# A hybrid decoder layer on one core: FF2's weight sums move into the stage of q and gates, rows and u stores change tiles and queues

## The chip, the cores and the metric

The kernel runs on one core of one Trainium2 chip. The time is device microseconds for one launch. Lower is better. Engines are named as in the profile: PE (TensorE), DVE (VectorE), ACT (ScalarE), POOL (GpSimd), SP (SyncE, which here only issues DMAs).

## The reference, cut to what matters

One layer on 2048 prompt tokens and 8 x 4 sampled tokens, width 1024, FF width 4096, all in float32:

```python
h = _rmsnorm(x, n1)
z = h @ w_in                                   # 1024 x 4864
hq, hf, hi, hg, sq, sk, sv, ga, gb = split(z)
y_a = (hgrn2(hq, hf, hi) normed * silu(hg)) @ w_up_a
y_b = sliding_window_attention(rot(sq), rot(sk), sv, sinks) @ w_up_b
m = sigmoid(ga) * y_a + sigmoid(gb) * y_b
x = x + m @ w_o
h2 = _rmsnorm(x, n2)
x = x + square(relu(h2 @ w_ff1)) @ w_ff2       # 1024 x 4096, 4096 x 1024
y = _rmsnorm(x, normf_w)
```

## The kernel before, in words

**Products.** Each float32 operand is split into a rounded high part (a cast on ACT, line 230) and a low part (a subtraction on DVE, line 231), and a product is three matmuls: high x high, high x low, low x high. A weight tile `r_...` of 128x1024 is loaded by SP's queue into the ring `w` (`wtile`, 12 tiles), and its parts `h_...` and `l_...` take two more tiles of it. The ring serves all of the kernel that needs a 128x1024 tile for a short time.

**Tokens.** Four blocks b0 to b3 of 512 tokens make two superblocks, sb0 (b0, b1) and sb1 (b2, b3; the samples ride along, so its halves have 528 columns in two chunks of 264). For each superblock the program has these stages:

1. Norm tiles (`norm_tile`): rows of x are normed, transposed on PE, and the transposed rows `hw` are kept for the even block in the slots `hT` (split) and written to DRAM as `hraw` for both.
2. `skv` and `sq`: keys, values and queries of attention for the even block (`colN`, `colN512`), staged in tiles `zqkb` and stored to DRAM (`zqk`). `sq` takes the eight rows of the weight in four steps of 24 matmuls; each step needs one `h_sqb` and one `l_sqb`.
3. The stage of q and gates (`strassen_T("z...")`): hq, gb and ga of both blocks at once by a seven-product Strassen scheme. Its operands: `hraw` comes back as `za11b` to `za22b` (ring `zs`), DVE forms `zs1b`, `zs2b` and differences, and these are split into the slots `zA`, `zS`. The weights `w1r_z` are loaded as 128x512 tiles, combined on DVE (lines 273 to 279) and split into `w1T_z`, `w1B_z`. A *unit* is one pair of columns of 128; there are ten. `a()` of a unit is its first two products (`fB`, `fC`), `b()` the next three (`fB`, `fD`, `fB`), `c()` the last two; a product is 12 matmuls. In sb0 the order is: `a` of units 0 to 5, `b` of unit 0, and then for each further unit `c` of the unit before and its own `b`, from unit 6 on with its own `a` ahead of both. Results are added up on DVE out of PSUM (lines 301, 314, 327, 335) and stored to DRAM (`z`) on the queues of POOL (q) and ACT (gates).
4. The even block: attention, HGRN2 with `hi`, `hf`, `hg`, gate b, gate a, then `wo`, and norm 2. The transposed rows `h2w` are written to `h2T`. During `wo` of the even block `reload` brings the odd half of `hraw` into `hT`. Then the odd block, with its own `sq` and `skv` at its head.
5. FF1 (`strassen_T("f...")`, 16 pairs): its results `u` are stored as seven operands for FF2 by `f1_fin`, on SP's queue.
6. FF2 in seven steps, whose weights are `w_ff` and four combinations of it, `w_T` (T1 to T4). The end forms the output rows (`Fin`: the final norm, tiles `nj` and `fx`).

**The weight sums.** The four combinations are made once, in sb0, by `w2_sums(i)` for i = 0 to 15: four loads of 128x512 (line 466, 256 KB each), four subtractions on DVE (lines 468 to 471), four stores (line 473). A ring `ws` of 5 tiles holds one sum; the fifth tile is the first difference. So the loads of sum i+1 wait until the stores of sum i have landed. In the program before, hooks in `sq` of b1, in the loops of the gates, and in the list of `reload` call them: they run from 285.8 to 556.6 us.

**The order of the work** on each engine is fixed when the program is built: a scheduler places the instructions by its own estimates, from the order of the code and the free tiles of the rings. At run time each engine and each queue takes its list strictly in order, so that an instruction that waits holds up all that stand behind it.

## Time and profile before

| what | value |
|---|---|
| three runs | 2969.36, 2987.56, 2986.71 us, median 2986.71 |
| profiled execution | 2976.32 us, its span 2974.5 us |
| mean granted TensorE clock | 0.979 |
| busy: PE, DVE, ACT, POOL | 95%, 60%, 40%, 10% |
| moved by DMA | 499 MB, mean 168 GB/s |

The profiled execution lies 10.4 us (0.35%) under the median of the three runs. The stages lie in it like this: norm tiles, skv and sq of sb0 up to about 84 us; the stage of q and gates 84 to 290; b0 to 507; sq and skv of b1 to 560; b1 to 790; FF1 to 1110; FF2 to 1459; sb1 the same way: sq of b2 and then the stage of q and gates from 1497 to 1703, b2 to 1940, b3 to 2278, FF1 to 2620, FF2 to the end. PE's busy time says little by itself, since a matmul at half clock counts double; the column PEclk goes with it.

### The profile page before, as it was taken

How to read it: one execution, taken by the hardware profiler on the slowest of the kernel's cores; microseconds unless marked ns; L12 is line 12 of the kernel's file. 1: busy time of each engine (PE TensorE's matmuls, PEld its weight loads, DVE VectorE, ACT ScalarE, POOL GpSimd, SP SyncE). 2: the span in 40 equal slices, each digit the busy share in tenths (PEclk: the TensorE clock that was granted, in tenths of full speed). 3: DMA queues.
4: the chain of work that ended last, by engine and by line, in shares of the span. 5: the costliest groups of instructions: out<-in, count | busy, mean ns of one | idle time of the engine just before them, and what ended most of it. 6: DMA issues, size and time to landing. Idle time of an engine off the chain costs nothing. (4 is left out here: it accounts for less than half of the span.)

```text
span 2974.5 us, 50416 instructions
## 1 busy us (share of the span) xinstructions
PE 2822.1 (95%) x20087; PEld 2444.8 (82%) x20087; DVE 1772.7 (60%) x2877; ACT 1179.3 (40%) x2257; POOL 291.3 (10%) x485
## 2 busy tenths in 40 slices
PE   5999998899999999999799999999998999999998
PEld 4877687777777888888699967777887999999998
DVE  4654785566677675545665457425756777654446
ACT  4434442434433344543343444234424333344433
POOL 4001011202200000010210010120012000000001
PEclk8999999999999999999899999999999999999999
DMA  7435757534644456665653423432256444485553
GB/s 238 156 121 167 231 192 268 182 97 139 217 162 152 154 196 237 228 214 191 214 150 106 140 93 98 155 123 87 84 182 187 152 144 155 141 284 199 176 194 107
DMA packets 417204, 499.08 MB, mean 168 GB/s; under 512 B 30636, under 2 KB 277448, under 8 KB 416952
## 3 DMA queue, kind: packets, MB, share of 16 engines
q1 hardware_dynamic: 380688, 411.12, 42.9%
q0 software_dynamic: 16448, 55.93, 5.7%
q10 hardware_dynamic: 19832, 28.79, 2.7%
q8 instruction: 158, 2.59, 0.4%
q14 instruction: 78, 0.64, 0.1%
HBM read 356.16 MB, written 140.61 MB: 167 GB/s over the span
## 5 line engine op out<-in xcount | busy, mean ns | idle before, releaser
L1324 PE MATMUL f<-f2S,hw2T 128*128 128x264 f32 (+1 forms) x576 | 184.1, 320 | 0.0
L1326 PE MATMUL f<-f2S,lw2T 128*128 128x264 f32 (+1 forms) x576 | 183.5, 319 | 0.0
L1325 PE MATMUL f<-f2S,hw2T 128*128 128x264 f32 (+1 forms) x576 | 183.5, 319 | 0.0
L155 DVE TENSOR_TENSOR lw2T<-lw2T,hw2T 128x1024 fp32r<-128x1024 f32 x64 | 78.1, 1223 | 121.1 <-ACT hw2T L154 120.7
L238 PE MATMUL fB_f<-S,w1T_f 128*128 128x264 f32 (+1 forms) x384 | 123.9, 323 | 6.0 <-DVE c_f L301 3.8
L1324 PE MATMUL f<-f2A,h_w2B 128*128 128x264 f32 (+1 forms) x384 | 123.3, 321 | 1.0 <-ACT f2A L154 1.0
L1325 PE MATMUL f<-f2A,h_w2B 128*128 128x264 f32 (+1 forms) x384 | 123.2, 321 | 0.9 <-DVE f2A L155 0.9
L240 PE MATMUL fB_f<-S,w1T_f 128*128 128x264 f32 (+1 forms) x384 | 123.0, 321 | 0.0
L239 PE MATMUL fB_f<-S,w1T_f 128*128 128x264 f32 (+1 forms) x384 | 122.9, 320 | 0.0
L1326 PE MATMUL f<-f2A,l_w2B 128*128 128x264 f32 (+1 forms) x384 | 122.7, 320 | 0.0
L154 ACT CAST hw2T<-lw2T 128x1024 fp32r<-128x1024 f32 x64 | 67.2, 1050 | 130.6 <-DMA lw2T<-w_T 128.7
L1324 PEld LDWEIGHTS f<-f2S,hw2T 128*128 128x128 f32 x576 | 108.4, 188 | 7.5 <-DVE hw_ab L410 0.3
L1325 PEld LDWEIGHTS f<-f2S,hw2T 128*128 128x128 f32 x576 | 108.4, 188 | 7.4
L1326 PEld LDWEIGHTS f<-f2S,lw2T 128*128 128x128 f32 x576 | 108.0, 188 | 7.6
L155 DVE TENSOR_TENSOR f2S<-f2S 128x1024 fp32r<-128x1024 f32 (+1 forms) x64 | 79.2, 1241 | 54.6 <-ACT f2S L154 53.5
L231 DVE TENSOR_TENSOR l_w2B<-rw2B,h_w2B 128x1024 fp32r<-128x1024 f32 x48 | 58.8, 1224 | 75.8 <-ACT h_w2B L230 69.9
L230 ACT CAST w1T_f<-w1r_f 128x512 fp32r<-128x512 f32 x128 | 76.4, 620 | 62.2 <-DVE w1r_f L275 29.5
L231 DVE TENSOR_TENSOR w1T_f<-w1r_f,w1T_f 128x512 fp32r<-128x512 f32 x128 | 85.9, 687 | 21.8 <-ACT w1T_f L230 21.4
L231 DVE TENSOR_TENSOR w1B_f<-w1r_f,w1B_f 128x512 fp32r<-128x512 f32 x96 | 65.4, 687 | 39.4 <-ACT w1B_f L230 38.5
L299 ACT COPY c_f<-fB_f 128x264 f32<-128x264 f32 (+1 forms) x80 | 36.0, 450 | 133.0 <-PE fB_f L240 130.3
L154 ACT CAST f2S<-f2S 128x1024 fp32r<-128x1024 f32 (+1 forms) x64 | 67.9, 1064 | 51.0 <-DMA f2S<-u_S 48.5
L191 PE MATMUL wob<-h_wob,m_b 128*128 128x512 f32 x192 | 76.6, 399 | 10.0 <-DVE ta_b L1023 10.0
(798 smaller groups left out, 9418.2 us busy)
## 6 DMA issues: line engine op xcount, KB each, us to landing
w1r_f<-w_ff SPq DMA_DIRECT2D x150, 256.0 KB
lw2T<-w_T SPq DMA_DIRECT2D x64, 512.0 KB
w1r_z<-w_in SPq DMA_DIRECT2D x102, 256.0 KB
rw2B<-w_ff SPq DMA_DIRECT2D x48, 512.0 KB
u_S<-s_f SPq DMA_DIRECT2D x128, 132.0 KB
f2S<-u_S SPq DMA_DIRECT2D x32, 528.0 KB
ws<-w_ff SPq DMA_DIRECT2D x64, 256.0 KB
r_wob<-w_o SPq DMA_DIRECT2D x32, 512.0 KB
```

What stands on the lines that cost most here:

```text
L154: nc.scalar.copy(hi, F(lo))
L155: nc.vector.tensor_tensor(lo, F(lo), F(hi), ALU.subtract)
L191: nc.tensor.matmul(ps[0:nr], lh, uh[:, kk, :], start=(k == 0), stop=False)
L230: nc.scalar.copy(dh, src)
L231: nc.vector.tensor_tensor(dl, src, F(dh), ALU.subtract)
L238: nc.tensor.matmul(ps, wh, ah, start=(first and k == 0), stop=False, skip_group_check=not first)
L239: nc.tensor.matmul(ps, wh, al, start=False, stop=False, skip_group_check=not first)
L240: nc.tensor.matmul(ps, wl, ah, start=False, stop=(last and k == 3), skip_group_check=not first)
L299: nc.scalar.copy(x, u.pB)
L1324: nc.tensor.matmul(ps, wh, ah, start=first, stop=False, skip_group_check=cont)
L1325: nc.tensor.matmul(ps, wh, al, start=False, stop=False, skip_group_check=cont)
L1326: nc.tensor.matmul(ps, wl, ah, start=False, stop=lastk, skip_group_check=cont)
```

## The change

- **Weight sums.** `w2_sums` takes its tiles from the pool of the stage of q and gates, and a new hook in `strassen_T`, called after each unit's `b()`, makes two sums for each of the first eight units of sb0. Loads and stores go to POOL's queue. The hooks in b0 and b1 are gone. The ring `st` of that stage has 11 tiles in sb0 and 31 in sb1 (16 and 32 before).
- **Rows.** In sb0 the transposed rows `hw` of the norm tiles go to tiles of the ring `zs` (14 tiles, with `za` and `zs`); the stage tiles of q, k, v are one view of slot 3 in both superblocks, in place of four tiles of the ring `w`. Slot 3 is also that of the operand S3 (`zS`). `skv` of the even block no longer calls the norm tiles of the odd half; the hook of `sq` and the loop behind it do. The output rows of the second half of sb0 share the slot of the first half, in place of four tiles of the ring `w`.
- **Gate a.** Eight loads on SP's queue into tiles `t4` become four loads of 512 KB on POOL's queue into slot 1. The next content of slot 1 (`hT` of the odd block, A12 of FF1) so comes behind the end of gate a.
- **h2w.** Both halves of a row tile share one tile `t4`.
- **u stores.** The stores of `f1_fin` go to POOL's queue.

```diff
+    def hw_zq(name):
+        junk = zq.tile([P, 1024], BF16, tag="junk", bufs=1, name="j" + name)
+        return junk, lambda half: zq.tile([P, Ths[0]], F32, tag="zs", bufs=14, name=f"{name}{half}")[:, 0:512]
...
-    def w2_sums(i):
+    def w2_sums(i, ws):
...
-                r[kh, nh] = wk.tile([P, 512], F32, tag="ws", bufs=5, name=f"ws{i}{kh}{nh}")
-                nc.sync.dma_start(r[kh, nh], w2[(kh * NP + i) * P:(kh * NP + i + 1) * P, nh * 512:(nh + 1) * 512])
+                r[kh, nh] = ws(f"ws{i}{kh}{nh}")
+                nc.gpsimd.dma_start(r[kh, nh], w2[(kh * NP + i) * P:(kh * NP + i + 1) * P, nh * 512:(nh + 1) * 512])
...
-            nc.sync.dma_start(wT[o][i * P:(i + 1) * P, :], x)
+            nc.gpsimd.dma_start(wT[o][i * P:(i + 1) * P, :], x)
...
-            stage = {}
+            stage = op(3, F32, f"zqk_{B}")[:, 0:768 * ncb].rearrange("p (c e) -> p c e", e=768)
...
-            colN(C_SQ + 512, f"skv{B}", st_skv, step)
+            colN(C_SQ + 512, f"skv{B}", st_skv)
             colN512(C_SQ, f"sq{B}", st_sq, lambda i: step())
...
+                def z_hook():
+                    for _ in range(2):
+                        if sums:
+                            w2_sums(sums.pop(0), lambda name: zp.tile([P, 512], F32, tag="ws", bufs=5, name=name))
...
-                           lambda ln, name: zp.tile([P, ln], F32, tag="st", bufs=16 * len(chunks), name=name),
-                           z_fin, 6 if len(chunks) == 1 else 10)
+                           lambda ln, name: zp.tile([P, ln], F32, tag="st", bufs=(11 if sb == 0 else 31), name=name),
+                           z_fin, 6 if len(chunks) == 1 else 10, z_hook)
...
-            colN512(C_SQ, f"sq{B}", ev_sq, lambda i: sum_next() if i % 2 else None)
+            colN512(C_SQ, f"sq{B}", ev_sq)
...
+        ga = op(1, F32, "ga_" + B)[:, 0:KD * T].rearrange("p (k t) -> p k t", k=KD)
+        for j in range(0, KD, 2):
+            nc.gpsimd.dma_start(ga[:, j:j + 2, :], zd[bi][(HH + KD + j) * P:(HH + KD + j + 2) * P, :].rearrange("(k p) t -> p k t", p=P))
...
-                nc.sync.dma_start(tas[0][:, 0:T], zd[bi][(HH + KD + j) * P:(HH + KD + j + 1) * P, :])
...
-                hw = t2(f"h2w_{B}_{c}_{half}").rearrange("p (k t) -> p k t", k=4)
+                if half == 0:
+                    hts[t, "w"] = t4(f"h2w_{B}_{c}")
+                hw = hts[t, "w"][:, half * 512:(half + 1) * 512].rearrange("p (k t) -> p k t", k=4)
...
-                    todo += [lambda g=g, k=k: reload(g, k), sum_next]
-            per = -(-len(todo) // (KD - 1))
+                    todo.append(lambda g=g, k=k: reload(g, k))
+            per = 1
...
-                    nc.sync.dma_start(us[o][u.n // 4][u.n % 4 * P:(u.n % 4 + 1) * P, u.t0:u.t0 + u.ln], y_)
+                    nc.gpsimd.dma_start(us[o][u.n // 4][u.n % 4 * P:(u.n % 4 + 1) * P, u.t0:u.t0 + u.ln], y_)
...
-                f1 = fin_list(1, None, None)
+                f1 = fin_list(1, nj, None)
```

What moves on the engines shows at three places. Line numbers are those of each program; the line of a sum's first subtraction is 468 before and 478 after.

**First place: DVE in the stage of q and gates of sb0.** In the program before, the list from the end of the third unit's weights on holds the weights of the next units and the adds out of PSUM (`c_z<-fD_z`), without a sum:

```order
L231 TENSOR_TENSOR w1B_z_2_1117<-w1r_z_2_1097,w1B_z_2_1117 128x512
L273 TENSOR_TENSOR w1r_z_3_1199<-w1r_z_3_1196,w1r_z_3_1193 128x512
L274 TENSOR_TENSOR w1r_z_3_1193<-w1r_z_3_1193 128x512
L275 TENSOR_TENSOR w1r_z_3_1199<-w1r_z_3_1196,w1r_z_3_1193 128x512
L279 TENSOR_TENSOR w1r_z_3_1196<-w1r_z_3_1196,w1r_z_3_1199 128x512
L327 TENSOR_TENSOR c_z_1_0_1090<-fD_z_1_0_1065,c_z_1_0_1090 128x512
L231 TENSOR_TENSOR w1T_z_3_1203<-w1r_z_3_1199,w1T_z_3_1203 128x512
```

In the changed program the same place has the sums 3 and 4 among these rows (`ws` are the tiles of a sum, line 478 its first and 481 its last subtraction):

```order
L478 TENSOR_TENSOR ws3t<-ws_1164,ws_1160 128x512
L231 TENSOR_TENSOR w1T_z_2_1191<-w1r_z_2_1181,w1T_z_2_1191 128x512
L335 TENSOR_TENSOR c_z_0_0_978<-fD_z_0_0_980,c_z_0_0_978 128x512
L479 TENSOR_TENSOR ws_1160<-ws_1160,ws_1158 128x512
L231 TENSOR_TENSOR w1T_z_2_1195<-w1r_z_2_1178,w1T_z_2_1195 128x512
L480 TENSOR_TENSOR ws_1164<-ws_1164,ws_1160 128x512
L231 TENSOR_TENSOR w1B_z_2_1198<-w1r_z_2_1178,w1B_z_2_1198 128x512
L481 TENSOR_TENSOR ws_1162<-ws_1162,ws_1164 128x512
L273 TENSOR_TENSOR w1r_z_3_1314<-w1r_z_3_1311,w1r_z_3_1308 128x512
```

Sum 4 begins seven rows further on. All 16 sums stand in this stage: the first behind the add of `fC` of unit 2 and the weights of units 3 to 5, the last (sum 15) six rows behind the add that ends `c` of unit 7; inside the first 15 sums stand 29 rows that are not theirs, as four do in sum 3 above.

**Second place: DVE at sq of b0.** In the program before, the low part of the second step of `sq` stands seven rows behind that of the first:

```order
L231 TENSOR_TENSOR l_sqb_457<-r_sqb_454,h_sqb_456 128x1024
L669 TENSOR_TENSOR za21b_589<-za11b_587,za21b_589 128x512
L670 TENSOR_TENSOR za12b_588<-za12b_588,zs2b_592 128x512
L231 TENSOR_TENSOR zS_0_583<-zs2b_592,zS_0_583 128x512
L231 TENSOR_TENSOR zS_0_582<-zs1b_591,zS_0_582 128x512
L231 TENSOR_TENSOR zS_0_584<-za21b_589,zS_0_584 128x512
L231 TENSOR_TENSOR zS_0_586<-za12b_588,zS_0_586 128x512
L231 TENSOR_TENSOR l_sqb_487<-r_sqb_484,h_sqb_486 128x1024
```

In the changed program the first, `l_sqb_374`, is followed by 25 rows of the operands of the stage of q and gates, and then the other three come together; these are the last of those rows:

```order
L679 TENSOR_TENSOR za12b_673<-za12b_673,zs2b_677 128x512
L231 TENSOR_TENSOR zS_0_596<-zs2b_677,zS_0_596 128x512
L231 TENSOR_TENSOR zS_0_595<-zs1b_676,zS_0_595 128x512
L231 TENSOR_TENSOR zS_0_599<-za12b_673,zS_0_599 128x512
L231 TENSOR_TENSOR l_sqb_428<-r_sqb_425,h_sqb_427 128x1024
L231 TENSOR_TENSOR l_sqb_482<-r_sqb_479,h_sqb_481 128x1024
L231 TENSOR_TENSOR l_sqb_536<-r_sqb_533,h_sqb_535 128x1024
L231 TENSOR_TENSOR w1B_z_0_703<-w1r_z_0_700,w1B_z_0_703 128x512
```

**Third place: ACT at the change from sb0 to sb1.** In the program before, the casts of `sq`'s weights of b2 stand behind those of the operand `zA`, which needs `za22b` out of DRAM:

```order
L205 ACTIVATE jkf_11305,fs_896_11748<-fx_896_11746 128x512
L649 COPY zqkb_11893<-ps_skvb_3_11868 128x256
L230 CAST zA_1_12030<-za22b_12035 128x528
L230 CAST zS_1_12027<-zs1b_12036 128x528
L230 CAST h_sqb_11901<-r_sqb_11899 128x1024
L230 CAST zS_1_12028<-zs2b_12037 128x528
```

In the changed program they stand among the squares of the output rows (`jkf,fs<-nj`), all ahead of `zA`:

```order
L230 CAST h_sqb_11941<-r_sqb_11939 128x1024
L205 ACTIVATE jkf_11292,fs_768_11707<-nj_11290 128x512 x2
L658 COPY zqk_b_11758<-ps_skvb_2_11823 128x256
L205 ACTIVATE jkf_11292,fs_896_11731<-nj_11290 128x512
L658 COPY zqk_b_11758<-ps_skvb_3_11849 128x256
L230 CAST h_sqb_11971<-r_sqb_11969 128x1024
L230 CAST zA_1_12010<-za22b_12015 128x528
L230 CAST w1B_z_0_12115<-w1r_z_0_12112 128x512
```

So `sq` of b2 no longer stands behind `za22b` on ACT; on DVE the low parts `l_sqb` of b2 move in the same way, and the first low part of the stage's weights, `w1B_z_0`, stands 23 rows behind the first row that uses `za22b`.

More of the change, by code (lines that the diff above doesn't have):

```diff
@@ L707, in tile_hybrid_step @@
             nc.gpsimd.dma_start(qS, zd[bi][0:HH * P, 0:NS].rearrange("(h p) t -> p h t", p=P))
-        sums = iter(range(8 * bi, 8 * bi + 8) if sb == 0 else ())
-        def sum_next():
-            i = next(sums, None)
-            if i is not None:
-                w2_sums(i)
         def ev_sq(ps, kind, c, nr):
```

46 lines of the change are left out of this document (20 added, 26 removed).

## The prediction

> **What bounds the kernel now.** I read the page first, then PE's waits, then the stretches in which they lie.
>
> ```profile
> span 2974.5 us, 50416 instructions
> ...
> PE 2822.1 (95%) x20087; PEld 2444.8 (82%) x20087; DVE 1772.7 (60%) x2877; ACT 1179.3 (40%) x2257; POOL 291.3 (10%) x485
> ...
> PEclk8999999999999999999899999999999999999999
> ```
>
> PE is busy for 2822.1 of 2974.5 us, so all idle time together is 152 us, and no edit here takes a matmul away. What can be won is a part of the idle time and of the stretches at a lower clock that stand beside it; what can be lost is new waits. The waits:
>
> ```profile
> PE ps_sqb L191 <- ACT h_sqb L230: 23.3, 2, 12.9
> PE tp_fb L225 <- DVE h2w_b L1104: 8.8, 3, 5.9
> PE fB_z L238 <- ACT c_z L299: 6.9, 4, 3.3
> PE ps_sqb L191 <- DVE y_b L1141: 5.9, 1, 5.9
> ```
>
> (columns: us in total, times, longest). The first is `sq` of b0 and of b2, the second and fourth lie at the head of b1. In stretches (length, PE, PEld, DVE, ACT, POOL busy, PEclk, DMA share, GB/s):
>
> ```profile
> 40.00:60.00 20.00, 4.94 (x32) 4.10 (x30) 3.37 (x6) 4.17 (x7) 10.68 (x19) 0.69 0.77 232
> 60.00:80.00 20.00, 18.95 (x75) 15.20 (x76) 20.00 (x31) 13.36 (x22) 3.89 (x8) 0.88 0.72 237
> 500.00:520.00 20.00, 14.10 (x51) 11.15 (x50) 7.52 (x10) 4.40 (x6) 1.49 (x4) 0.83 0.90 323
> 540.00:560.00 20.00, 12.11 (x76) 11.70 (x75) 10.40 (x14) 4.27 (x6) 6.69 (x11) 0.74 0.84 264
> 1460.00:1480.00 20.00, 8.23 (x23) 6.35 (x24) 11.36 (x17) 7.66 (x12) 7.37 (x14) 0.57 0.88 301
> 1920.00:1960.00 40.00, 40.00 (x175) 30.79 (x175) 10.12 (x10) 14.52 (x19) 4.77 (x11) 1.00 0.54 173
> 140.00:160.00 20.00, 15.77 (x68) 12.26 (x67) 11.80 (x18) 6.15 (x12) 1.62 (x3) 1.00 0.28 92
> 180.00:200.00 20.00, 20.00 (x89) 16.36 (x88) 11.78 (x18) 6.78 (x11) 0.00 (x0) 1.00 0.34 109
> 85.00:285.00 200.00, 193.88 (x849) 158.56 (x849) 102.74 (x152) 79.46 (x135) 10.06 (x19) 1.00 0.44 141
> ```
>
> The stage of q and gates (85 to 285 us), into which the sums go, is PE-bound now: 6.1 us idle of 200, DVE busy for half. The head of b1 (500 to 560), which they leave, is not.
>
> **The head of b1: a gain of 20 us.** Idle there: 20.00 - 14.10 and 20.00 - 12.11, together 13.8 us. The clock of 0.83 and 0.74 takes 0.17 x 20 + 0.26 x 20 = 8.6 us more, 22.4 in all. The transition from b2 to b3 does the same work without sums, and PE is busy there for 40.00 of 40.00 us at clock 1.00. The sums stood in DVE's list and in SP's between the loads of `sq` and `skv`, and the four rows `h2w` of the ring `t2` get tiles of twice the size. Bounds: 0 and -22.4. I take -20, near to the row of b3, since DVE has the same list there. If the 256 KB loads of `sq` were what PE waits for, the gain would be some 6 us, the wait for `y_b`.
>
> **sq of b2: a gain of 13 us.** ACT and DVE before:
>
> ```profile
> 1464.48 0.63 ACT L230 CAST zA<-za22b 128x528 fp32r<-128x528 f32 x1 [5.25 <-DMA za22b<-hraw]
> ...
> 1470.67 1.04 ACT L230 CAST h_sqb<-r_sqb 128x1024 fp32r<-128x1024 f32 x1 [4.74 <-DMA r_sqb<-w_in]
> ...
> 1471.77 1.65 PE L191 MATMUL ps_sqb<-h_sqb,hT 128*128 128x512 f32 x3 [12.94 <-ACT h_sqb L230]
> ...
> 1475.98 0.70 DVE L667 TENSOR_TENSOR zs1b<-za21b,za22b 128x528 f32<-128x528 f32 x1
> 1476.60 1.22 DVE L231 TENSOR_TENSOR l_sqb<-r_sqb,h_sqb 128x1024 fp32r<-128x1024 f32 x1
> ...
> 1496.95 0.28 PE L238 MATMUL fB_z<-hT,w1B_z 128*128 128x264 f32 x1
> ```
>
> PE waits 12.94 us for the first weight, which is loaded late (its tiles are free only when output rows leave the ring) and stands behind `zA`. The clock of 0.57 costs 0.43 x 20 = 8.6 us beside it. With the rows out of the ring and the casts ahead of `zA`, `sq` runs from 1458.8 (1471.77 - 12.94) for 96 matmuls of 20.00/89 = 0.225 us, to 1480.4. Then another thing is late: `w1B_z_0` stands 23 rows behind the first row on `za22b` (1464.5, as now, since the loads of `za` stay where they are). At 0.62 us a row (1475.98 to 1476.60) that is 14.3 us, with the 1.5 us or so for which the next tiles land later 1480 to 1482, and its second half five rows further, 1485. So the stage begins at about 1482 and waits some 2 us more: 1484 against 1496.95, -13. Bounds: 0 and -21.5. If the loads come late as now, nothing is won.
>
> **sq of b0: a loss of 9 us.**
>
> ```profile
> 59.50 0.69 DVE L667 TENSOR_TENSOR zs1b<-za21b,za22b 128x512 f32<-128x512 f32 x1 [8.08 <-DMA za22b<-hraw]
> ...
> 61.31 1.22 DVE L231 TENSOR_TENSOR l_sqb<-r_sqb,h_sqb 128x1024 fp32r<-128x1024 f32 x1
> ...
> 66.06 1.22 DVE L231 TENSOR_TENSOR l_sqb<-r_sqb,h_sqb 128x1024 fp32r<-128x1024 f32 x1
> ...
> 67.80 0.68 DVE L231 TENSOR_TENSOR zA<-za22b,zA 128x512 fp32r<-128x512 f32 x1
> 68.40 0.68 DVE L668 TENSOR_TENSOR zs2b<-zs1b,za11b 128x512 f32<-128x512 f32 x1
> ```
>
> Now a step of `sq` starts every 4.75 us (61.31, 66.06), and its 24 matmuls take 24 x 0.225 = 5.4 us: DVE keeps up. After the change 25 rows of 0.60 us (67.80 to 68.40) lie between the first low part and the second, 15 us, so PE waits about 10 us after the first step; the half-clock stretch that follows such a wait (the clock of 0.69 beside the wait of 10 us here) is already in the time before. Against it the ring's free tiles bring the first weight and `hraw` earlier, by up to 5 us (I take 4, and 3 more from the wait at the first step, now counted as one). 15 - 4.75 + 3 - 4 = 9. What follows it does not give this back: the operands that DVE makes early are not waited for now (20 us of 20 in 60 to 80 on DVE, and PE at 193.88 of 200 afterwards). Bounds: -3, if DVE's early rows are done before PE gets to `sq`, and +15.
>
> **The sums in the stage of q and gates: a loss of 25 us.** In work this fits: 64 subtractions of 0.69 us are 44 us on a DVE that idles for 97 of 200, and 128 transfers of 256 KB lie beside a DMA share of 0.44. What does not fit is the chain of a sum:
>
> ```profile
> L466 SPq DMA_DIRECT2D ws<-w_ff x64: 328/432/1009, 285.8 to 539.9; - x64
> ...
> L473 SPq DMA_DIRECT2D w_T<-ws x48: 319/326/1076, 300.1 to 556.6; - x48
> ...
> L666 POOL DMA_DIRECT2D za21b<-hraw x8: 536/537/622, 54.9 to 1475.7; - x8
> ...
> L468 DVE TENSOR_TENSOR ws9t<-ws,ws x1: 683/683/683, 469.9 to 469.9; 128x512 f32<-128x512 f32 x1
> ...
> 522.78 0.69 DVE L468 TENSOR_TENSOR ws13t<-ws,ws 128x512 f32<-128x512 f32 x1 [7.88 <-DMA ws<-w_ff]
> ...
> 524.96 0.69 DVE L471 TENSOR_TENSOR ws<-ws,ws 128x512 f32<-128x512 f32 x1
> ...
> 533.63 0.69 DVE L468 TENSOR_TENSOR ws14t<-ws,ws 128x512 f32<-128x512 f32 x1 [7.98 <-DMA ws<-w_ff]
> ```
>
> With five tiles, sum 14 begins 533.63 - 522.78 = 10.85 us after sum 13, of which DVE stands idle for 7.98: last subtraction, store, landing, load, landing. On POOL's queue the store and the two loads on that chain issue in 0.54 us against 0.33 and 0.43: +0.4. The 29 foreign rows inside 15 sums add 29 x 0.60 / 15 = 1.2. So a sum takes 12.4 us; from sum 9 to 13 it took (522.78 - 469.9)/4 = 13.2. What PE grants: the first sum stands behind the add of product 6 of the stage, the last behind that of product 58 (12 for `a` of six units; then 3, and 5 or 7 for each further unit). A product is 12 x 0.225 = 2.7 us: 52 x 2.7 = 140, with six rows behind the add 144, or 9.6 us for each of 15 steps. The list of DVE is in order, and behind a waiting sum stand the low parts of the weights and the adds that empty PSUM; those adds may be late by about one to three products (3 to 8 us: `fD` must be read before `c` writes it again). So 15 x (12.4 - 9.6) = 42 less 8 is the loss if each transfer lands as at 523 to 533, where the DMA share was high; if it lands in 2 us less, 12. I take 25, nearer to the first since the share will be high: 0.34 in 180 to 200 and the 2.1 MB of a sum in 12 us, 175 GB/s beside 109. No clock loss is added: in 140 to 160 PE idles for 4.2 us at clock 1.00. Bounds: 0 and +60 (14.3 us a sum, as from sum 12 to 13: 15 x 4.7 = 70 less 8).
>
> "DMAs initiated by the scalar, sync or gpsimd engine will ultimately run on the same 16 DMA engines", says the Trainium skill, DMA: Bandwidth & Descriptors, "Issuing engines are not separate DMA queues": POOL's queue buys issue slots on SP and no transfer time. The same page's "Specifications" put the limit of the memory at about 358 GB/s; the 323 GB/s of the stretch 500 to 520 comes near to it, and the 284 that I expect would stay clear, so by the page alone transfers would not slow down and the loss would be the lower 12.
>
> **The rest: a gain of 2 us.**
>
> ```profile
> SPq L1227 <- DVE c_f L1211: 185.5, 92, 6.0
> ...
>   ACT c_f L1215: 4.3, 2
>   ACT c_f L299: 2.5, 1
> ...
> PE wob L191 <- DVE ta_b L1023: 10.0, 4, 2.7
> ```
>
> SP stands for 185.5 us behind the u stores (L1227), but who waited for those is ACT for 6.8 us. POOL takes 336 of them (16 and 32 units, seven each) at the 0.54 us of L666, 181 us of the 660 that the two stages of FF1 last; the weights' loads, freed on SP, make PE wait little now. Bounds -7 and +3, value -2. The loads of gate a are covered by gate b; slot 1 then comes later, but `wo` lies ahead of its next use (8 rows x 4 tiles x 2 halves x 3 = 192 matmuls, 43 us), and the wait for `ta_b` stays. Were that cover gone, an odd block would wait for one landing of 512 KB. The `h2w` tiles are counted above. 0.
>
> **Sum.** -20 - 13 + 9 + 25 - 2 = -1 on an execution of 2976.3 us. Since that lies 10.4 us under the median of the runs, I give 2980: no difference that this measurement can tell. (1% is 30 us; the three runs lie 18 us apart, so less than about 1% can't be told from no change.)
>
> **Rivals.** (1) *The sums fit* (0.20). If a sum keeps to 9.6 us, the stage of q and gates stays at its length; the start loses 4 at most: -20 - 13 - 2 + 2 = -33, to -40: 2940. For it: DVE idles for half. Against it: no step in the trace under 10.8 us. (2) *The chain of a sum decides* (0.22): 14.3 us a sum, as with 323 GB/s in flight, +60; the loads of attention for b0 stand behind the last sum on POOL's queue and come late, +4 in place of the covered 0; the start at +12. -35 + 76 = +41: 3017 to 3025. It decides from about 13.8 us a sum on. (3) *The head of b1 stays* (0.08), because its weights' loads, not the sums, are late: -6 in place of -20: 2995. The likeliest, all terms as above: 0.50, with its own range 2960 to 3000.
>
> **Range and chances.** The low end takes in rival 1 but for its tail, the high end rival 2: 2942 to 3025. Faster by over 1% (under 2957): 0.20, rival 1. Slower (over 3016): 0.20, most of rival 2. The rest 0.60.
>
> **What would show it.** In the profile after: PE idle of at most 4 us between 480 and 560 and a clock near 1.0 there; `ps_sqb` of b2 without the wait for `h_sqb`, and a wait of `fB_z` for `w1B_z` of some us in its place; at the start a wait of `ps_sqb` for `l_sqb` of about 10 us; in the stage of q and gates waits of DVE for `ws` of 1 to 4 us with each sum, and PE waiting for DVE's `w1T_z`, `w1B_z`, `c_z`. I am wrong if steps of a sum on POOL's queue are much shorter than on SP's, if PE's slack against DVE is larger than 8 us, or if POOL's own work at the start of a stage (norms) is held up by its stores.

## The result, and the profile after

The changed kernel takes 2995.7 us (median of 10 runs, 2991.0 to 3004.6), the kernel before 2977.0 us (median of 10, 2969.4 to 2987.6): a ratio of 1.0064, with a 95% interval from 1.0047 to 1.0081. It is slower by about 19 us, where the prediction saw no difference; the time lies inside the predicted range of 2942 to 3025 us. The profiled execution of the changed kernel took 3003.1 us, 7 us over its median, that of before 0.7 us under its median as the ten runs give it; so the two profiles lie 27 us apart, of which some 8 are scatter. (The median of 2986.7 us in the table at the top was that of three runs.)

The stage of q and gates of sb0 shows the difference. Below stand its rows in the stretches view, first of before, then of the changed kernel (length, PE, PEld, DVE, ACT, POOL busy, PEclk, DMA share, GB/s):

```profile
85.00:277.00 192.00, 185.88 (x816) 152.37 (x816) 99.58 (x149) 76.31 (x131) 6.47 (x12) 1.00 0.42 134
```

```profile
87.00:320.00 233.00, 199.44 (x814) 159.81 (x813) 135.96 (x211) 75.47 (x131) 74.40 (x138) 0.93 0.76 247
...
545.00:595.00 50.00, 49.14 (x303) 42.54 (x303) 18.98 (x25) 23.00 (x36) 16.84 (x32) 1.00 0.55 168
1477.00:1510.00 33.00, 23.61 (x101) 18.36 (x100) 20.09 (x32) 15.06 (x28) 9.58 (x19) 0.89 0.84 267
1717.00:1737.00 20.00, 12.26 (x62) 9.85 (x60) 4.45 (x5) 5.89 (x10) 6.59 (x12) 0.86 0.73 239
```

The stage has become 41 us longer (from its first matmul to that of `hi` of b0: 192.4 before, 233.7 after). PE, at clock 1.00 and idle for 6 us before, idles for 33.6 us at clock 0.93. PE's busy time grows by 13.6 us for the same matmuls (199.44 against 185.88 us). Neither DVE (136 of 233) nor the transfer engines (0.76) are full. The head of b1 (545 to 595) is as forecast: PE 49.14 of 50, clock 1.00. The waits of PE over the whole kernel, in the changed kernel (us in total, times, longest):

```profile
PE fB_z L238 <- ACT c_z L299: 21.4, 7, 6.8
PE ps_sqb L191 <- ACT h_sqb L230: 21.1, 2, 12.5
PE fD_z L238 <- DVE c_z L327: 8.5, 4, 5.9
...
PE fB_z L238 <- ACT zqk_b L661: 6.8, 1, 6.8
...
PE qT_b2c L757 <- POOL qkv_b L754: 6.4, 1, 6.4
PE fD_f L238 <- DVE c_f L327: 6.3, 3, 2.4
```

The waits for `h2w` and `y_b` at the head of b1 are gone. The first and third stand nearly all in the stage of q and gates of sb0 (19.7 and 7.6 us of them), the second at `sq` of b0. The last three lie in sb1 and in FF1 and are new or longer (the wait of `qT_b2c` was 2.0 us before). The first row means that PE waits for ACT to copy a result out of PSUM. ACT's list is held up in its turn, most by casts that wait for DVE:

```profile
ACT w1T_z L230 <- DVE w1r_z L275: 47.5, 10, 11.6
```

And what DVE waits for, in the stage:

```profile
DVE w1r_z L273 <- DMA w1r_z<-w_in: 16.4, 4, 10.5
...
DVE ws12t L478 <- DMA ws<-w_ff: 5.8, 1, 5.8
DVE ws9t L478 <- DMA ws<-w_ff: 5.4, 1, 5.4
...
DVE ws2t L478 <- DMA ws<-w_ff: 4.4, 1, 4.4
```

and so on for most of the 16 sums, 49 us together (all waits for `ws<-w_ff` in the stage added up). A sum begins 13.1 us after the one before on the mean of 15 (106.2 to 302.3 us), where the forecast had 12.4.

Where the time went, by the first matmuls of each stage in the two profiles: start to the stage of q and gates +1.8 us; that stage +41.3; b0 with its `wo` -7.1; head of b1 (`sq` to `hi`) -13.9; b1 -2.9; FF1 +1.7; FF2 up to the output rows -2.5; output rows and `sq` of b2 -8.5; stage of q and gates of sb1 +4.1; b2 +6.1; b3 with its head -4.8; FF1 +4.7; FF2 to its last matmul +4.5; together 24.5 of the 26.8.

### The profile page after: what moved, and what is told of

It reads as the page before. It is cut to its first block, busy times and chain, and to the rows that moved or that the text cites. A ratio compares the mean times of both kernels' runs of the same rounds, so it can differ in the third digit from the quotient of the medians.

```text
span 3001.4 us, 50568 instructions
## 1 busy us (share of the span) xinstructions
PE 2829.8 (94%) x20087; PEld 2447.6 (82%) x20087; DVE 1767.1 (59%) x2877; ACT 1176.6 (39%) x2257; POOL 550.6 (18%) x965
## 4 chain that ended last, share of the span: by engine, by line
PE 70%; DMA 13%; DVE 6%; issue 4%; POOL 3%; ACT 2%; SPq 1%; ACTq 0%; DVEq 0%; POOLq 0%
PE f L1326 6%; PE f L1325 6%; PE f L1324 6%; PE fB_f L238 3%; PE fB_f L240 3%; PE fB_f L239 3%; DMA ws<-w_ff 2%; PE fD_f L238 2%; PE fD_f L240 2%; PE fD_f L239 2%; DMA w1r_f<-w_ff 1%; PE wob L191 1%; PE wob L192 1%; PE wob L193 1%; DMA w_T<-ws 1%
## 5 line engine op out<-in xcount | busy, mean ns | idle before, releaser
L1325 PE MATMUL f<-f2S,hw2T 128*128 128x264 f32 (+1 forms) x576 | 183.5, 319 | 0.0
L1229 POOL DMA_DIRECT2D u_S<-s_f x192 | 103.3, 541 | 141.1 <-DVE s_f L1224 106.7
L1229 POOL DMA_DIRECT2D u_A<-c_f x104 | 56.2, 541 | 216.4 <-DVE c_f L1213 215.0
L238 PE MATMUL fB_z<-zS,w1T_z 128*128 128x264 f32 (+1 forms) x240 | 79.6, 332 | 17.2 <-ACT c_z L299 13.2
```

The costliest lines, as they stand in the source:

```text
L238: nc.tensor.matmul(ps, wh, ah, start=(first and k == 0), stop=False, skip_group_check=not first)
L1229: nc.gpsimd.dma_start(us[o][u.n // 4][u.n % 4 * P:(u.n % 4 + 1) * P, u.t0:u.t0 + u.ln], y_)
L1325: nc.tensor.matmul(ps, wh, al, start=False, stop=False, skip_group_check=cont)
```

## Experiments: which part, and where

All times below are medians, and a ratio is that to the kernel before in the same series, with its 95% interval. Stage lengths are from the profile of each kernel, from the first matmul of `fB_z` to the first of `hi` of b0. Each is one execution: sp_order, sp_order_u and sp_order_u_qbd (below) have the same lists of DVE and ACT in this stage and 213.8, 211.3 and 217.4 us, so a difference of some 6 us between two kernels tells nothing.

**The sums back in b0 and b1 (sums_back).**

```diff
-                           z_fin, 6 if len(chunks) == 1 else 10, z_hook)
+                           z_fin, 6 if len(chunks) == 1 else 10)
...
+            colN512(C_SQ, f"sq{B}", ev_sq, lambda i: sum_next() if i % 2 else None)
```

> The changed kernel with the weight sums back in the hooks of b0 and b1, on SP's queue, with tiles of the block's pool; all other parts of the change stay. Theory (the chain of a sum on five tiles sets the pace of the stage of q and gates): that stage falls from 233.7 to 192-196 us. If the sums made the waits at the head of b1, the stretch from sq of b1 to hi of b1 goes back from 37.4 to 48-52 us; if the tiles of h2w made them, it stays under 40. Total 2965-2975 in the first case, 2950-2960 in the second. Rival (the other parts of the change cost as much as they gain): over 2977.

2978.2 us, ratio 1.0000 (0.9985 to 1.0015). The stage is back at 195.5 us, as expected. The other parts of the change, all of them together, gain nothing: the rival (over 2977 us) holds, by 1 us.

```profile
519.00:567.00 48.00, 41.21 (x234) 36.38 (x232) 23.81 (x30) 19.67 (x28) 14.44 (x26) 0.93 0.85 287
```

That is the head of b1 in this kernel: 47.1 us long, a little under the 48 to 52 expected, with PE idle for 6.8 us. So most of the gain there belongs to the sums.

**The move of the sums alone (sums_only).** The kernel before with the hook, POOL's queue and the smaller ring `st`.

```diff
-                           z_fin, 6 if len(chunks) == 1 else 10)
+                           z_fin, 6 if len(chunks) == 1 else 10, z_hook)
...
-            colN512(C_SQ, f"sq{B}", ev_sq, lambda i: sum_next() if i % 2 else None)
+            colN512(C_SQ, f"sq{B}", ev_sq)
```

> The kernel before with the move of the weight sums alone (hook in the stage of q and gates, POOL's queue, ring st of 11 and 31). Theory: the stage of q and gates grows from 192.4 to 228-236 us; the head of b1 (sq to hi, 51.4 us) falls to under 42 if the sums made its waits and stays near 50 if h2w did. Total 2995-3000 in the first case, 3010-3020 in the second. Rival (the stage suffers from the other parts that share POOL's queue and the slots): stage under 215, total under 2985.

3006.5 us, ratio 1.0100 (1.0073 to 1.0127). The stage has 238.3 us (+45.9), the head of b1 39.2 (-12.2; PE 38.90 of 40 us):

```profile
84.00:321.00 237.00, 199.39 (x812) 159.98 (x811) 138.11 (x213) 75.44 (x130) 73.84 (x137) 0.91 0.77 250
553.00:593.00 40.00, 38.90 (x234) 34.23 (x233) 13.57 (x15) 16.22 (x23) 14.45 (x27) 1.00 0.51 159
```

The sums, not `h2w` or the loads, made the waits at the head of b1, and the move alone costs the whole loss and more. The total lies 6.5 us over the span given for that case, and the stage 2 us over its own.

**Half of the sums in the stage (sums_split).**

```diff
-                    for _ in range(2):
+                    for _ in range(1):
```

and sums 8 to 15 in the hooks of b0.

> The changed kernel with one sum per unit for eight units in the stage of q and gates, and the other eight in the hooks of b0 only. Theory (a sum takes 13 us, PE grants 9.6 at two per unit and 13.7 to 19 at one): stage 192-202 us, head of b1 as in the changed kernel (37), b0 as before (184-188): total 2955-2965, under both kernels. Rival (any sum in that stage slows its weights' loads): stage 212 or more, total over 2975.

2996.0 us, ratio 1.0069 (1.0044 to 1.0095): missed. The scheduler put the eight sums at nearly the same times as the first eight of the changed kernel (105 to 206 us), so a hook once per unit did not spread them; the stage has 214.1 us, 21.7 more than before for half of the sums, and b0 from `hi` to `wo`, with the other eight on POOL's queue there, has 205.9 us in place of 183.5.

**The sums on SP's queue (sums_sp).**

```diff
-                nc.gpsimd.dma_start(r[kh, nh], w2[(kh * NP + i) * P:(kh * NP + i + 1) * P, nh * 512:(nh + 1) * 512])
+                nc.sync.dma_start(r[kh, nh], w2[(kh * NP + i) * P:(kh * NP + i + 1) * P, nh * 512:(nh + 1) * 512])
...
-            nc.gpsimd.dma_start(wT[o][i * P:(i + 1) * P, :], x)
+            nc.sync.dma_start(wT[o][i * P:(i + 1) * P, :], x)
```

> The changed kernel with the loads and stores of the weight sums on SP's queue, still in the stage of q and gates. Theory (ring and landing set the chain; SP saves 0.4 us a sum): stage 224-236 us, total 2986-3000. Rival (POOL's queue: its 0.54 us issues, its waits for the stores of z, and few transfers in flight): stage under 212, total under 2976. Other way: SP's queue puts the weights' loads of the stage behind waiting sums, stage over 240.

2966.6 us, ratio 0.9972 (0.9955 to 0.9989): the rival was right, and my theory, which gave POOL's queue 0.4 us a sum, fell. The same sums in the same stage, on the other queue:

```profile
86.00:291.00 205.00, 194.65 (x816) 156.96 (x815) 136.00 (x211) 75.17 (x131) 6.46 (x12) 0.96 0.87 285
```

The stage has 205.4 us, 28 less than with POOL's queue, for the same 136 us of DVE and the same bytes. The higher share (0.87 at 285 GB/s against 0.76 at 247) is the shorter stage told in other words: share times length is 178 us here and 177 us in the changed kernel, so the transfers themselves keep their engines busy for as long on either queue. A sum begins every 11.2 us. One step of it on SP's queue, DVE and SP:

```profile
126.80 0.69 DVE L481 TENSOR_TENSOR ws<-ws,ws 128x512 f32<-128x512 f32 x1
...
136.41 0.69 DVE L478 TENSOR_TENSOR ws3t<-ws,ws 128x512 f32<-128x512 f32 x1 [2.56 <-DMA ws<-w_ff]
```

```profile
126.07 1.77 SPq L483 DMA_DIRECT2D w_T<-ws  x3
127.89 3.16 SPq L476 DMA_DIRECT2D ws<-w_ff  x4
```

and one of the changed kernel on POOL's:

```profile
218.15 0.69 DVE L481 TENSOR_TENSOR ws<-ws,ws 128x512 f32<-128x512 f32 x1
...
229.26 0.69 DVE L478 TENSOR_TENSOR ws9t<-ws,ws 128x512 f32<-128x512 f32 x1 [5.44 <-DMA ws<-w_ff]
```

```profile
219.14 0.54 POOL L483 DMA_DIRECT2D w_T<-ws  x1
220.11 0.54 POOL L476 DMA_DIRECT2D ws<-w_ff  x1 [0.43 <-DMA w_T<-ws]
223.26 0.54 POOL L476 DMA_DIRECT2D ws<-w_ff  x1 [2.61 <-DMA w_T<-ws]
```

From the end of the last subtraction to the last load's issue there are 4.4 us on POOL's queue (218.84 to 223.26), of which 2.61 and 0.43 are waits for stores to land; the first subtraction of the next sum comes 10.4 us after the last one's end, against 8.9 us on SP's queue (127.49 to 136.41). Over all 15 steps, a step falls apart like this (means in us):

| part of a step | changed kernel | sums_sp |
|---|---|---|
| first subtraction's start to last one's end | 3.9 | 3.7 |
| to the last store's issue | 0.3 | 0.1 |
| to the last load's issue | 3.3 | 2.5 |
| to the next first subtraction | 5.5 | 5.0 |

In the steps in which DVE waits for a load, the last part has 5.2 us in the changed kernel and 5.1 in sums_sp: the loads land no later on POOL's queue. The largest part of the 1.9 us, 0.8, lies between the last store and the last load.

The edit changes one thing more than the queue. The scheduler also places DVE's rows anew: inside the first 15 sums stand 21 rows that are not theirs in sums_sp, and 29 in the changed kernel. No run held the order fixed. But the order alone does not make the difference: sp_order (below) has 38 such rows on SP's queue and 213.8 us, sums_only 24 on POOL's and 238.3.

## Experiments: why POOL's queue

**Another order of the four loads (pool_order, sp_order).** The tile that the last store frees is loaded last, since only the last subtraction reads it.

```diff
-        for kh in range(2):
-            for nh in range(2):
+        for kh, nh in ((0, 0), (0, 1), (1, 1), (1, 0)):
```

> The changed kernel with the four loads of a sum in another order: the tile that the last store frees is loaded last, so the first subtraction no longer waits for it (its two tiles are freed by the second and third store). All on POOL's queue. Theory (the stage grows by 15 times what a sum takes over 9.6 us, less 11 us): a sum takes 11.2-11.9 us in place of 13.1, stage 205-216 us (233.7 in the changed kernel), total 2968-2980. Rival (POOL's queue or the shared transfer engines slow the weights' loads, whatever the chain): stage over 225, total over 2988.

> Loads and stores of the sums on SP's queue, and the other order of the four loads. Theory: a sum takes 9.5-10.2 us in place of 11.2, stage 192-198 us (205.4 with SP's queue alone), total 2953-2961. Rival (what is left over 192 is the work of the sums on DVE or the transfer engines): stage stays at 203-206, total 2964-2968.

pool_order: 2998.7 us, ratio 1.0091 (1.0069 to 1.0112), stage 235.9. sp_order: 2972.6 us, ratio 0.9999 (0.9985 to 1.0013), stage 213.8. Both missed, and on SP's queue the new order is worse than the old one (205.4). In pool_order a sum begins every 12.5 us instead of 13.1 and the stage is no shorter, so the rule on which I had put the numbers (15 times what a sum takes over 9.6 us, less 11) is not one: the scheduler also places the subtractions elsewhere, more of DVE's other rows stand inside a sum (4.7 us from the first to the last subtraction, 3.9 before), and DVE waits 59 us for `ws` instead of 49.

**Loads and stores on two queues (mix_loads_pool, mix_stores_pool).** One of the two edits of sums_sp each.

> The changed kernel with only the loads of the sums on POOL's queue and their stores on SP's. Open: what on POOL's queue makes the stage 28 us longer than on SP's (233.7 against 205.4). Theory A (the stores: on POOL's queue they land 4.4 us after their issue on the mean, and the next loads stand behind them in the same list): stage 204-214, total 2966-2976. Theory B (the loads: 0.54 us each and 5.2 us to landing): stage 225-235, total 2988-2998. If each has a share: 215-224.

> The changed kernel with only the stores of the sums on POOL's queue and their loads on SP's. Theory A (stores): stage 225-235, total 2988-2998. Theory B (loads): 204-214, total 2966-2976. If each has a share, 215-224; if loads and stores in one list hold each other up, both mixed kernels lie under 210.

mix_loads_pool: 3012.6 us, ratio 1.0131 (1.0103 to 1.0159), stage 252.2. mix_stores_pool: 2990.8 us, ratio 1.0067 (1.0043 to 1.0091), stage 238.5. With the loads alone on POOL's queue the stage is longer than in the changed kernel, with the stores alone as long within the scatter (and the ratios agree, 1.0067 and 1.0064). So neither the loads nor the stores alone carry the cost of POOL's queue, and putting them in one list is not what does it either. None of the theories holds.

**One queue for the whole stage, and the two queues exchanged (all_pool, weights_pool).** The first puts the weights of sb0's stage on POOL's queue too, the second only these, with the sums on SP's:

```diff
-                nc.sync.dma_start(v[:, i], u.src(u.n, *b).rearrange("(k p) c -> p k c", p=P))
+                (nc.gpsimd if u.N.startswith("z0") else nc.sync).dma_start(v[:, i], u.src(u.n, *b).rearrange("(k p) c -> p k c", p=P))
```

> The changed kernel with the loads of the weights of sb0's stage of q and gates on POOL's queue too, so that this stage has one queue for weights and sums. Theory 1 (two queues at once make each other's transfers land late): stage 205-218 us, total 2968-2982. Theory 2 (POOL's queue is slower by itself: issues of 0.54 us, later landings): stage 232 or more, total over 2994.

> The sums' transfers on SP's queue and the weights of sb0's stage of q and gates on POOL's: again two queues, the other way round. Theory 1 (two queues): stage 228 us or more, total over 2988. Theory 2 (POOL's queue slow by itself, the sums' chain is what counts): stage 200-212, total 2960-2972, as with all on SP's.

all_pool: 2996.6 us, ratio 1.0077 (1.0050 to 1.0103). weights_pool: 2985.1 us, ratio 1.0037 (1.0026 to 1.0048). Their stages, in this order:

```profile
87.00:324.00 237.00, 199.06 (x814) 156.02 (x813) 135.22 (x212) 74.38 (x131) 108.00 (x183) 0.94 0.75 248
```

```profile
86.00:319.00 233.00, 200.63 (x816) 159.97 (x815) 137.07 (x212) 76.41 (x132) 39.29 (x56) 0.93 0.75 249
```

237.8 and 233.3 us. One queue does not help as long as it is POOL's: theory 2 holds in all_pool, which speaks for a slower POOL queue. With the sums on SP's and the weights on POOL's the stage is long as well, and a sum on SP's queue takes 12.6 us: there theory 1 holds (with the total 3 us under its bound), which speaks for the two queues hindering each other. The profile gives the landing of POOL's transfers alone (a store of a sum in the changed kernel):

```profile
DMA to landing us min/median/max: 2.3/3.7/5.9
```

For SP's there is no such row, so the landings of the stores can't be compared; the 3.3 us from the last store's issue to the last load's, against 2.5 in sums_sp, fit with later landings on POOL's queue and do not prove them. The profile also lists the queues under two kinds (packets, MB, share of 16 engines; POOL's and SP's queue in the stage, first the changed kernel, then sums_sp):

```profile
q0 software_dynamic: 10801, 35.54, 45.7%
q1 hardware_dynamic: 24320, 13.63, 20.9%
```

```profile
q1 hardware_dynamic: 42752, 47.20, 72.1%
q0 software_dynamic: 768, 2.79, 3.5%
```

The sums' bytes go in fewer and larger packets on POOL's queue, and a MB keeps the engines busy for some 3 us on either. So it is not the packets that are slower.

**ACT's queue in place of POOL's (mix_stores_act, mix_loads_act, weights_act).** The three splits again, with `nc.scalar` where mix_stores_pool, mix_loads_pool and weights_pool have `nc.gpsimd`.

```diff
-            nc.gpsimd.dma_start(wT[o][i * P:(i + 1) * P, :], x)
+            nc.scalar.dma_start(wT[o][i * P:(i + 1) * P, :], x)
```

> The changed kernel with the loads of the sums on SP's queue and their stores on ACT's. If it is POOL's queue itself that lowers the rate, the stage of q and gates has 203 to 217 us, as with all three streams on SP's, and at most 10 more for casts of ACT that stand behind a waiting store: total 2962 to 2980. If any second queue beside SP's hinders it, the stage has 233 us or more, as with the stores on POOL's (238.5), total 2985 to 2996.

> The changed kernel with the loads of the sums on ACT's queue and their stores on SP's. By the theory of POOL's queue the stage has 205 to 225 us (a load waits for stores to land, and ACT's casts stand behind it; ACT idles for two thirds of the stage), total 2964 to 2985. By the theory of a second queue 240 us or more, as with the loads on POOL's (252.2), total 2990 to 3015.

> The sums on SP's queue, and the weights of sb0's stage on ACT's. By the theory of POOL's queue the stage has 205 to 225 us, total 2964 to 2980; by the theory of a second queue 233 us or more, as with these weights on POOL's (233.3), total 2983 to 2996.

2988.8, 2985.5 and 2985.1 us, ratios 1.0058 (1.0037 to 1.0080), 1.0045 (1.0030 to 1.0060) and 1.0038 (1.0025 to 1.0051). The stages have 230.2, 230.0 and 227.6 us: all three miss the spans of the theory of POOL's queue, and stay 3 to 10 us under those of a second queue. By the totals, mix_stores_act and weights_act lie in the spans of a second queue, mix_loads_act in neither. And by the ratios ACT's queue does as POOL's for the weights (1.0038 and 1.0037) and, within the intervals, for the stores (1.0058 and 1.0067); only the loads are better on ACT's (1.0045 and 1.0131). The stretches view of the first and the last:

```profile
85.00:315.00 230.00, 200.36 (x817) 160.94 (x816) 135.42 (x212) 74.44 (x131) 6.46 (x12) 0.93 0.77 253
```

```profile
85.00:312.00 227.00, 196.39 (x815) 158.06 (x814) 136.78 (x212) 75.93 (x132) 6.47 (x12) 0.94 0.79 258
```

DVE's waits for `ws`, all added up in the stage, are 54, 49 and 37 us with the stores, the loads and the weights on POOL's queue, and 31, 18 and 22 us with them on ACT's; in the six kernels with all on SP's they are 24 to 38, 29 in sums_sp. So DVE does not wait longer for a sum with ACT's queue. That does not make the transfers as early as on SP's queue: from the last store's issue to the last load's there are 3.2 to 3.6 us in the three kernels with ACT's queue, 3.5 to 3.9 in the three with POOL's, and 2.5 in sums_sp. What is late with ACT's queue, besides, is ACT itself, whose casts and copies stand behind transfers that wait. In mix_stores_act (PE and ACT in the stage):

```profile
PE fB_z L238 <- ACT c_z L299: 25.3, 7, 5.0
...
ACT c_z L299 <- DVE ws L481: 14.2, 2, 7.3
```

The second row is copies out of PSUM that stood behind the stores of a sum, and such a store waits for its subtraction. The first row alone proves little, since it has 19.7 us in the changed kernel too (4.4 in sums_sp). So these runs do not tell how much a second queue as such costs; the weights and the stores, which cost the same on POOL's and on ACT's, speak for it, and the loads do not. What is shown: with all three streams (weights, loads and stores of sums) on SP's queue the stage has 203 to 217 us; with any of them on POOL's 233 us or more, and DVE waits 8 to 25 us longer for the sums' tiles than in sums_sp (30 in pool_order); with any on ACT's 228 us or more, and there DVE does not wait longer for the sums' tiles. Why the stage is longer with any queue but SP's stays open. The Trainium skill, SBUF — State Buffer, "Who interferes with whom", warns that transfers issued from GpSimd can starve while DVE copies or casts, and says that a probe saw `tensor_copy` stall them and `tensor_tensor` not. Each of the 211 DVE rows of the stage is a TENSOR_TENSOR, so by that page this is unlikely to be the cause here; no run changed it.

## Experiments: the other parts, and a kernel under both

**The u stores (sp_order_u), and the zero tile (sp_order_u_qbd).**

```diff
-                    nc.gpsimd.dma_start(us[o][u.n // 4][u.n % 4 * P:(u.n % 4 + 1) * P, u.t0:u.t0 + u.ln], y_)
+                    nc.sync.dma_start(us[o][u.n // 4][u.n % 4 * P:(u.n % 4 + 1) * P, u.t0:u.t0 + u.ln], y_)
```

> As sp_order, and the u stores back on SP's queue. Theory (the u stores on POOL's queue cost FF1 some us: 323.5 and 351.5 us in the changed kernel, 318.7 and 347.4 where only the sums moved): FF1 318-322 and 346-348, total 2-6 us under sp_order. Rival (prediction: they gain 2 us): FF1 as in sp_order or longer.

2961.9 us, ratio 0.9960 (0.9946 to 0.9975), 10.6 us under sp_order: more than expected. FF1 has 316.2 and 347.5 us (322.5 and 350.8 in sp_order). In the changed kernel PE waits in FF1 for 6.3 us for `c_f` (row above); here that row is gone, and DVE waits for FF1's weights for 8.1 us in sb0's FF1 in place of 16.4 (15.6 in sp_order):

```profile
DVE w1r_f L273 <- DMA w1r_f<-w_ff: 16.4, 4, 5.1
```

```profile
DVE w1r_f L273 <- DMA w1r_f<-w_ff: 8.1, 4, 3.0
```

(first the changed kernel, then sp_order_u). So the u stores on POOL's queue cost time in FF1, and in sb0's the weights on SP's queue come later with them; in sb1's this wait stays at 5 us. sums_u_sp (below) repeats it against sums_sp: 6.1 and 2.5 us less in the two FF1.

In b2 of the changed kernel a memset of a tile of the samples, which the scheduler had moved up, stands on POOL ahead of the rotation of the queries:

```profile
1722.25 0.36 POOL L752 TENSOR_TENSOR r_b2c<-qkv_b,rot 128x80 f32<-128x80 f32 x1
1731.45 1.06 POOL L784 MEMSET qbd<- 128x1152 f32 x1 [8.85 <-DMA r_hfb<-w_in]
1732.47 1.38 POOL L753 TENSOR_TENSOR qkv_b<-qkv_b,rot 128x160 f32<-128x160 f32 x1
```

```diff
-            nc.gpsimd.memset(qbd, 0.0)
+            nc.gpsimd.tensor_scalar(qbd[:, 0:1024], kcT, 0.0, 0.0, ALU.mult, ALU.add)
+            nc.gpsimd.tensor_scalar(qbd[:, 1024:DB * 144], kcT[:, 0:DB * 144 - 1024], 0.0, 0.0, ALU.mult, ALU.add)
```

> As sp_order_u, and the zero tile qbd of the samples' queries is made from another tile of b3 (times 0.0) in place of a memset, so that it cannot stand ahead of the rotation of b2's queries on POOL's queue. Theory (the memset waits 9 us for a store of the stage of q and gates whose tile lay at the same place, and holds up the rotation behind it): b2 from hi to wo falls from 196 to 185-189 us, total 6-10 us under sp_order_u. Rival (the rotation waits for its own loads): no change.

2962.8 us, ratio 0.9967 (0.9952 to 0.9981), as sp_order_u. The memset no longer stands there, the rotation ends earlier, and the transposes wait 4.7 us all the same. That wait ends when ACT copies the transposes before them out of PSUM, and this copy stands behind a cast that waits for a weight of `hf`:

```profile
1708.84 1.04 ACT L230 CAST h_hfb<-r_hfb 128x1024 fp32r<-128x1024 f32 x1 [5.14 <-DMA r_hfb<-w_in]
1709.79 0.58 ACT L757 COPY SV_b<-qT_b2c 128x512 f32<-128x512 f32 x1
```

The theory fell. What makes b2 longer than before (6 us) as a whole is not settled.

**A kernel under both (sums_u_sp), and a longer ring (sums_u_sp_ring7).** The changed kernel with the sums and the u stores on SP's queue and the loads in the first order; and the same with other rings in sb0:

```diff
-                            w2_sums(sums.pop(0), lambda name: zp.tile([P, 512], F32, tag="ws", bufs=5, name=name))
+                            w2_sums(sums.pop(0), lambda name: zp.tile([P, 512], F32, tag="ws", bufs=7, name=name))
...
-                           lambda ln, name: zp.tile([P, ln], F32, tag="st", bufs=(11 if sb == 0 else 31), name=name),
+                           lambda ln, name: zp.tile([P, ln], F32, tag="st", bufs=(9 if sb == 0 else 31), name=name),
```

> The changed kernel with the sums' transfers and the u stores on SP's queue, and the loads of a sum in the first order. From the runs so far: stage 205, FF1 316-319 and 347-349, total 2953-2960: under the kernel before by 0.5 to 0.8%. Rival (the two gains do not add, since SP's queue is then full in FF1 and in the stage): 2964 or more.

> As sums_u_sp, with 7 tiles for the sums and 9 for the results (ring st) of the stage, so that two loads of the next sum need not wait. Theory (the five tiles set what a sum takes): 10.3 us or less a sum (11.2 now), stage 194-201. Rival (DVE's own work of 139 us and the weights' loads set the stage now): stage 203-212, whatever the ring.

sums_u_sp: 2955.4 us, ratio 0.9943 (0.9923 to 0.9963), stage 205.0, FF1 317.1 and 347.0: the gains add. It is faster than the kernel before by about 16 us, and than the changed one by about 36 (by the two ratios, since the series differ). sums_u_sp_ring7: 2954.0 us, ratio 0.9934 (0.9912 to 0.9956), stage 202.6. A sum takes 10.3 us, as expected, but the stage gives only 2.4 us back, which is within the scatter and at the edge of the rival's span. DVE is busy for 136 of the 202 us there and still waits 24 us for the sums' tiles and 8 for the stage's own weights; which of these sets the rest is not shown.

## Why the prediction was wrong, step by step

**The head of b1: right.** -20 forecast, -21.0 measured for b0 with `wo` and the head together (b0 up to `wo` +2.0, `wo` -9.1, the head -13.9). sums_only and sums_back give most of it to the sums.

**The sums in the stage: the mechanism right, the size not.** The failing step is "42 less 8 is the loss if each transfer lands as at 523 to 533 ...; if it lands in 2 us less, 12. I take 25". It was 41. (The 12 leaves out the 8 that the other end subtracts; with it, the lower end is 4.) POOL's queue was sized by its issue time alone (+0.4 us a sum from 0.54 against 0.33 and 0.43); sums_sp shows 1.9 us a sum, and 28 us of the 41 in the stage, for the queue with the order that the scheduler makes for it. The rest, 13 us, stays with the sums on SP's queue too; the forecast named the chain on five tiles and DVE's work for it, and no run separates them (two tiles more took 2.4 us off). With the 13.1 us that a sum took in place of 12.4, the forecast's own line gives 15 x (13.1 - 9.6) = 52 less 8 = 44, and with the 11.2 of sums_sp 24 less 8 = 16, against 41 and 13 measured: the line holds for these two. In the other kernels with all sums in the stage it lies between 4 us too high (weights_act) and 12 too low (mix_loads_pool), so it is a rough guide. What failed is the price of a step on POOL's queue and the choice of 25 between its two results. "No clock loss is added" is open: PE's busy time in the stage grew by 13.6 us at a clock of 0.93, and no run shows how much of that would have been waiting anyway. And PE waited mostly for ACT's copies (19.7 us), behind casts that waited for DVE, where the forecast had it wait for DVE itself. Bandwidth did not decide: the stretch has 247 GB/s, and sums_sp moves 292 GB/s from 100 to 280 us in a stage 28 us shorter.

The Trainium skill, DMA: Bandwidth & Descriptors, "Specifications", with its limit of about 358 GB/s, had spoken for the lower 12. The stretches shown here stay under that limit (292 GB/s over 180 us, 323 over 20 us), and the loss came in spite of it. The same page of the Trainium skill, "Issuing engines are not separate DMA queues", says that issuing from several engines saves time on the sequencer only; the forecast took from it that POOL's and SP's queue do the same apart from issue slots. Here the measurement differs and decides: the stage has 205.4 us with the sums on SP's queue and 233.7 on POOL's.

**sq of b0: mis-sized.** +9 forecast, +1.8 measured. The order of DVE does what was described, and PE waits twice:

```profile
50.96 1.65 PE L191 MATMUL ps_sqb<-h_sqb,hT 128*128 128x512 f32 x3 [12.49 <-ACT h_sqb L230]
...
67.67 1.22 PE L191 MATMUL ps_sqb<-h_sqb,hT 128*128 128x512 f32 x2 [8.60 <-ACT h_sqb L230]
```

The first wait was there before (10.36 us). The second is the forecast one: the cast that ends it stands in ACT's list behind casts of `zS`, which wait for the 25 rows of DVE; the low part that the forecast named begins at 67.75 us, just behind. `sq` grew by 11.8 us, near to the 13 forecast (15 - 4.75 + 3). The term that failed is the 4 us for what the freed ring brings earlier: `sq` starts at 51.0 us in place of 61.0.

**sq of b2: right in kind, smaller.** -13 forecast, -8.5 measured. `sq` begins as forecast: 1477.05 us, where the forecast has 1458.8 and FF2 ended 18.4 us later. The wait that takes the old one's place is longer than the 2 us given to it:

```profile
1506.81 0.59 PE L238 MATMUL fB_z<-hT,w1B_z 128*128 128x264 f32 x1 [6.83 <-ACT zqk_b L661]
```

The stage's first product waits for ACT to empty PSUM of `sq`; that copy stands behind the casts of `zS` in ACT's list. The forecast looked at `w1B_z` alone, for whose low part PE then waits 2.35 us more. The step that failed is "1464.5, as now": with the 18.4 us added, the first row on `za22b` would be at 1482.9, and it came 5 us later. The 23 rows behind it took 21.3 us in place of 14.3, since DVE waited 7 us among them for a cast of ACT:

```profile
1487.92 0.71 DVE L676 TENSOR_TENSOR zs1b<-za21b,za22b 128x528 f32<-128x528 f32 x1 [4.18 <-DMA za22b<-hraw]
...
1498.08 0.71 DVE L231 TENSOR_TENSOR zS<-zs2b,zS 128x528 fp32r<-128x528 f32 x1 [6.98 <-ACT zS L230]
...
1509.23 0.68 DVE L231 TENSOR_TENSOR w1B_z<-w1r_z,w1B_z 128x512 fp32r<-128x512 f32 x1
```

**The rest: wrong in sign.** -2 forecast for FF1, +6.4 measured in its two stages; sp_order and sp_order_u differ by 10.6 us in all. The step "the weights' loads, freed on SP, make PE wait little now" failed: with the u stores on POOL's queue these loads came later in sb0's FF1 (DVE waits 15.6 us for them in sp_order, 8.1 in sp_order_u). b2 (+6) was in no term.

**The sum.** Against the profiled -1 forecast and +27 measured: the stage +16, FF1 +8, sq of b2 +4.5 and b2 +6 more than forecast, the start 7 less, and b3 5 less; that is 23 of the 28. So some 35 us of misses one way and 12 the other partly cancel, and that the time stayed inside the range is in part luck. sums_back shows that the gains outside the stage are used up by losses outside it; sums_only shows the stage's loss without them.

## What to carry to other kernels

A transfer that is moved to another queue is not only an issue slot: read how long a step of its chain takes on that queue, and what the other queues' loads do meanwhile, and where the trace has neither, put the upper end of the range into the forecast rather than its middle. Work that fits a stage by busy time may still not fit its order: find the shortest step that the chain ever took in the trace (10.85 us here), compare it with what the stage grants (9.6 us), and take the difference at its full size. When a move loses, try it with the old queue before undoing it: here the place was good, and the queue was not.

## What was not expected of the hardware

With all of the stage's streams on SP's queue, 292 GB/s were moved from 100 to 280 us at a DMA share of 0.89 (sums_sp, below), and 285 GB/s over the stage (268 to 288 in the six such kernels); with any one of them on POOL's queue it was 229 to 250 GB/s over the stage, though DVE and POOL had room, and on ACT's 253 to 258. The bytes are nearly the same in all, so these rates are the lengths of the stage in another unit. The same stores of FF1 cost about 10 us more on POOL's queue than on SP's, with POOL busy for a fifth of that stage in sb0 and a third in sb1.

```profile
100.00:280.00 180.00, 169.65 (x705) 136.24 (x704) 124.64 (x195) 62.56 (x111) 3.24 (x6) 0.95 0.89 292
```
